# A hybrid decoder layer on one core: index transposes two blocks further behind, two more table blocks ahead, and a reordered last stage

## The chip, the core and the metric

The kernel runs on one core of a Trainium2 chip. The metric is device time in microseconds of one execution, and the median over several executions is compared. In the profile PE is the matmul engine (TensorE) and PEld its weight loads, DVE is VectorE, ACT is ScalarE, POOL is GpSimd, SP is the engine that issues most of the table loads.

## The reference, cut to what matters

The layer is an attention and recurrence mixer followed by PEER, a retrieval of single-neuron experts: each of 256 tokens picks, for each of 8 heads, 16 of 16,384 experts, and mixes their rows. The change touches only PEER and the final RMSNorm.

```python
q = (xt @ w_q).reshape(n, PEER_HEADS, 2, PEER_QDIM // 2)
s = jnp.einsum('nhpd,phkd->nhpk', q, sub_keys)
s1, i1 = lax.top_k(s[:, :, 0], K)          # K = 16 of 128 keys, twice
s2, i2 = lax.top_k(s[:, :, 1], K)
comb = s1[..., :, None] + s2[..., None, :]
cand = i1[..., :, None] * PEER_NKEYS + i2[..., None, :]
top_s, pos = lax.top_k(comb, K)
experts = jnp.take_along_axis(cand, pos, axis=-1)
gate = jax.nn.softmax(top_s, axis=-1)
a = jax.nn.gelu(jnp.einsum('nd,nhkd->nhk', xc, u_tab[ec]))
y = jnp.einsum('nhk,nhkd->nd', gc * a, v_tab[ec])
x = x + gt_f * y
out = x * rsqrt(mean(x * x) + EPS) * g_final
```

## The kernel before, in words

**Dense tokens and sparse tokens.** For the first 160 tokens (`DT`) the kernel computes all experts. The u table (128 blocks of 512 KB, each 128x1024 floats) is multiplied block by block with the layer input, which gives `pu`; a GELU goes into the large tile `W`; `W` is multiplied by a matrix of gates; then the v table (128 more blocks) is multiplied by `W` into `Y`. For the last 96 tokens, in two groups of 64 and 32 (`SPARSE`), expert rows are gathered: 96 gathers of 128 rows (512 KB each) from the u table, then 96 from the v table, issued on POOL into four buffers (`gat`), three ahead. DVE reduces each gathered u tile to one number per row (L1116), and adds each gathered v tile, scaled, into `hrow` (L1125 and L1127), one `hrow` for each group.

**The two loops.** The u loop and the v loop each run over k = 0 to 127. In each step PE does 8 matmuls of 128x160 with one table block. Table loads are issued by `table_ahead()`, one in a step, mostly on SP and about one in five on ACT; ten buffers (tags `raw` and `hl`) go round, and some early blocks have tiles of their own (`GB`, `tab2`, `tab3`).

**Work beside the u loop.** A chain of generators (`work`) holds the DVE work of choosing experts: `topk(1)`, `gates(1)`, `topk(0)`, `gates(0)`, `g_phase`. In each step `spend(work, more)` takes pieces from it until the costs that the pieces yield have used up an allowance of 2.5, less 1.27 for each gather step of that loop step; an overdraft or a remainder carries over. Gather steps come at 0.75 for each u step (`RATE`) and at one for each v step. This order in the program is the order in each engine's queue; an engine takes its instructions in order.

`gates(tt)` normalises the gates on DVE (its last operation is L1048), and then has PE transpose the two index tiles and the gate tile of 128 tokens (`pidx`, L1057 to L1059). `g_phase` builds one-hot matrices from the transposed indices on DVE and ACT (`od`, `oe`, `oa`, `ob`), multiplies them on PE (`pG`), and multiplies the result into `W` (L1167).

**The last stage.** After the v loop `fold` matmuls add the two groups' `hrow` into `Y`. For each of 8 tiles j: fold (PE), gate and residual `x2` (DVE, L1356), square (ACT, L1358), two transposes to rows (PE, L1347), and column sums of squares through matmuls with a column of ones (PE, `psq`). Then come the inverse root (L185 to L192), the scaling, and four stores.

Of the kernel before, what the change touches and what calls it, by code (L numbers as in the profile page):

```python
# [11 lines left out]
F32 = mybir.dt.float32  # L12
# [5 lines left out]
OP = mybir.AluOpType  # L18
AX = mybir.AxisListType

P = 128
# [58 lines left out]
def hybrid_block(ctx: ExitStack, tc: tile.TileContext, A):  # L80
# [47 lines left out]
    def ps(name):  # L128
        return psum.tile([P, 512], F32, name=name, tag="s", bufs=2)
# [618 lines left out]
    def table_ahead():  # L748

        n = len(held)  # L750
        if n >= len(tabs):
            return
        i = turn[n]
        if 6 <= i < 10:

            if i % 2 == 0:
                extra[0] = base.tile([P, 2, WMAX], F32, name="tab2", tag="H", bufs=2)
            r = extra[0][:, i % 2]
        elif 18 <= i < 22:

            r = extra[1].tile([P, WMAX], F32, name="tab3", tag=("oa", "ob")[i % 2], bufs=2)
        else:
            tag = "raw" if (n - (4 if n < 14 else 22)) % 10 in (0, 1, 2, 6) else "hl"
            r = stream.tile([P, WMAX], F32, name="tab", tag=tag, bufs=4 if tag == "raw" else HL)
        (nc.scalar if i >= 32 and i % 5 == 1 else nc.sync).dma_start(r, tabs[i])
        held[i] = r
# [275 lines left out]
    def gates(tt):  # L1042
        s = slice(tt * P, (tt + 1) * P)
        sel, g, gs = mine[tt][7].rearrange("p (a n) -> p a n", a=2), mine[tt][8].rearrange("p (h k) -> p h k", h=8), mine[tt][9]
        nc.vector.tensor_reduce(gs, g, axis=AX.X, op=OP.add)
        nc.vector.reciprocal(gs, gs)
        nc.vector.tensor_scalar(gs, gs, GS, None, op0=OP.mult)
        nc.vector.tensor_tensor(g, g, gs[:, :, None].to_broadcast([P, 8, 16]), op=OP.mult)  # L1048
        yield 0.6
        if tt == NT - 1:  # L1050
            for i, w in enumerate(SPARSE):
                nc.vector.tensor_copy(own[i][:, 1],
                                      g.rearrange("p h k -> p (h k)").rearrange("p (j g) -> p g j", g=P // w))
            spread(1, 0, 1)
        yield 1.4
        pt = ps("pidx").rearrange("p (a t) -> p a t", a=4)
        nc.tensor.transpose(pt[:, 0], sel[:, 0], ident)  # L1057
        nc.tensor.transpose(pt[:, 1], sel[:, 1], ident)
        nc.tensor.transpose(pt[:, 2], g.rearrange("p h k -> p (h k)"), ident)  # L1059
        yield 0.0  # L1060
        nc.scalar.activation(n1T[:, s], pt[:, 0], AF.Copy, scale=-1.0)
        nc.scalar.copy(i2T[:, s], pt[:, 1])
        nc.scalar.copy(gth[:, s], pt[:, 2])
        yield 1.4
        nc.vector.tensor_tensor(gtl[:, s], pt[:, 2], gth[:, s], op=OP.subtract)
        yield 0.3
# [191 lines left out]
    for k in range(P):  # L1258
# [3 lines left out]
        for dt in range(ND):  # L1262
            mm(o[:, k % 2], r[:, dt * P:(dt + 1) * P], h2[:, dt, :DT], dt == 0, dt == ND - 1)
        if k == 7:
            while len(held) < 22:
                table_ahead()
        if k == 8:
            while len(held) < 24:
                table_ahead()
        if 10 <= k < 18 or k >= 22:  # L1270
            table_ahead()
        if k % 2:
            gelu(k - 1, o)
# [47 lines left out]
    out_sb = tail[:, 3072:5120].rearrange("p (a c) -> p a c", a=NT)  # L1321
    sq = tail[:, 5120:7168].rearrange("p (a t) -> p a t", a=ND)
    st = pe.tile([P, 32], F32, name="st")
    for k in range(P):
        for j in range(ND):
            part(j, k, k == 0 and j % 2 == 0, k == P - 1)
        table_ahead()
        due[0] += 1.0
        while due[0] >= 1:
            due[0] -= 1  # L1330
            advance(rows)
        if k == 40:
            nc.sync.dma_start(gfin, bass.AP(tensor=A["g_final"].tensor, offset=A["g_final"].offset,
                                            ap=[[0, P], [1, D]]))
            preload(AF.Abs_reciprocal_sqrt)
# [10 lines left out]
                R[n, b] = (pa if n == 0 else ps)("pr").rearrange("p (a c) -> p a c", a=4)  # L1346
            nc.tensor.transpose(R[n, b][:, j % 4], x2[:, j, n * P:(n + 1) * P], ident)  # L1347

    def sums_of(i):
        for n in range(NT):  # L1350
            mm(psq[:, n:n + 1], sq[:, order[i], n * P:(n + 1) * P], ones[:, 0:1], i == 0 and n == 0, i == ND - 1)

    for i, j in enumerate(order):
        for g, n in enumerate(SPARSE):
            mm(Y[j // 2][:, j % 2, t_of[g]:t_of[g] + n], hrow[g][:, j * P:(j + 1) * P], fold[g], False, True)
        nc.vector.scalar_tensor_tensor(x2[:, j], Y[j // 2][:, j % 2], mod[:, 5, j:j + 1], xT[:, j], op0=OP.mult,  # L1356
                                       op1=OP.add)
        nc.scalar.activation(sq[:, j], x2[:, j], AF.Square)  # L1358
        if i == 2:
            psq = py("psq")  # L1360
        if i > 0:
            rows_of(i - 1)
        if i == 4:
            sums_of(0)
        if i > 3:
            sums_of(i - 3)
        if i == 5:
            for n in range(NT):
                nc.vector.tensor_tensor(out_sb[:, n, :512], R[n, 0].rearrange("p a c -> p (a c)"), gfin[:, :512],
                                        op=OP.mult)  # L1370
    rows_of(ND - 1)
    for i in (5, 6, 7):
        sums_of(i)
    ms, r, t = (st[:, 2 * i:2 * i + 2] for i in range(3))
    rsqrt_to(r, ms, t, psq[:, 0:NT], 1.0 / D)
    for n in range(NT):
# [86 lines left out]
```

## Time and profile before

| | us |
|---|---|
| median of 3 runs (lowest, highest) | 947.3 (947.17, 953.04) |
| the profiled execution's own time | 949.38 |
| its span, first to last instruction | 947.4 |
| PE busy in it | 916.0 |
| DVE busy in it | 642.6 |

The profiled execution took 1.98 us more than its span, and 2.1 us more than the median. The span falls into the mixer and the query projection (0 to some 324 us), the u loop (324 to 637), the v loop (637 to 919) and the last stage (919 to 947). Times in the rows below count from the span's start.

### The profile page before, as it was taken

To read this page: it belongs to the slowest core of one execution; us is meant where nothing else is said; L and a number is where in the kernel's file an instruction comes from. 1 tells how busy PE (TensorE), PEld (TensorE's weight loads), DVE (VectorE), ACT (ScalarE), POOL (GpSimd) and SP (SyncE) were. 2 spreads that over 40 slices of the span, in tenths; PEclk is the share of its full clock that TensorE was granted. 3 is DMA by queue.
4 is the path that set the end of the run, shared out by engine and by line. 5 is a ranking of instruction groups with operands and counts; after the bars stand their busy time and mean duration, and the time that the engine had idled before them with its cause. 6 is when DMAs were issued, how large, how long until landed. Compare 5 with 4: busy or idle time off the path is not lost.

```text
span 947.4 us, 17397 instructions
## 1 busy us (share of the span) xinstructions
PE 916.0 (97%) x6794; PEld 884.1 (93%) x6794; DVE 642.6 (68%) x1428; ACT 313.6 (33%) x693; POOL 216.9 (23%) x233
## 2 busy tenths in 40 slices
PE   6999999999999999999799999999999999999986
PEld 5899988779998999999799999999999999999986
DVE  7798848866878979888978888454444444444453
ACT  4384338865554522101487765010000000000002
POOL 1000000000001023632432333333333333333330
PEclk8999969999999999999899999999999999999995
DMA  9878445246659879899999999999999999999981
GB/s 351 335 267 257 171 131 181 89 141 239 204 180 381 324 270 355 306 418 418 341 373 347 360 337 369 406 417 419 419 417 419 418 419 419 419 417 419 418 325 44
DMA packets 86193, 306.43 MB, mean 323 GB/s; under 512 B 9984, under 2 KB 10464, under 8 KB 85984
## 3 DMA queue, kind: packets, MB, share of 16 engines
q1 hardware_dynamic: 50256, 176.24, 49.5%
q0 software_dynamic: 29520, 106.02, 28.8%
q10 hardware_dynamic: 6336, 23.07, 6.1%
q8 instruction: 53, 0.87, 0.4%
q14 instruction: 28, 0.23, 0.1%
HBM read 304.14 MB, written 1.05 MB: 322 GB/s over the span
## 4 chain that ended last, share of the span: by engine, by line
PE 44%; DMA 29%; DVE 13%; issue 9%; POOL 3%; ACT 0%; DVEq 0%; POOLq 0%; SPq 0%; ACTq 0%
DMA gat<-in_v_row_dram,pairs 24%; PE pu L118 10%; PE col L118 9%; DMA gat<-in_u_row_dram,pairs 5%; PE row L118 4%; PE pq L118 4%; POOL gat L1090 3%; DVE hrow L1127 3%; DVE gat L1116 3%; PE pout L118 2%; PE pbr L118 2%; PE po L118 2%; PE pS L118 2%; PE pG L118 1%; PE ph L118 1%
## 5 line engine op out<-in xcount | busy, mean ns | idle before, releaser
L118 PE MATMUL Y<-gb,tab 128*128 128x160 f32 x2048 | 280.6, 299 | 1.1 <-DMA tab<-in_v_row_dram 0.9
L118 PEld LDWEIGHTS Y<-gb,tab 128*128 128x128 f32 x2048 | 278.5, 190 | 3.2 <-DMA tab<-in_v_row_dram 2.0
L118 PE MATMUL pu<-h,tab 128*128 128x160 f32 x1984 | 278.3, 301 | 0.0
L118 PEld LDWEIGHTS pu<-h,tab 128*128 128x128 f32 x1984 | 272.7, 191 | 0.0
L1127 DVE SCALAR_TENSOR_TENSOR hrow<-gat,act,hrow 128x1024 f32<-128x1024 f32 x94 | 120.7, 1284 | 140.5 <-DMA gat<-in_v_row_dram,pairs 140.4
L1090 POOL DMA_INDIRECT gat<-in_u_row_dram,pairs x96 | 107.1, 1115 | 183.8 <-DVE gat L1116 132.3
L1116 DVE SCALAR_TENSOR_TENSOR gat<-gat,hrow 128x1024 f32<-128x1024 f32 x96 | 116.3, 1220 | 28.7 <-DMA gat<-in_u_row_dram,pairs 24.0
L1090 POOL DMA_INDIRECT gat<-in_v_row_dram,pairs x96 | 90.8, 946 | 181.6 <-DVE hrow L1127 170.2
L100 DVE TENSOR_TENSOR lo<-raw,hi 128x1024 fp32r<-128x1024 f32 (+2 forms) x67 | 80.5, 1206 | 17.8 <-ACT hi L99 17.8
L99 ACT CAST hi<-raw 128x1024 fp32r<-128x1024 f32 (+2 forms) x67 | 68.8, 1036 | 29.3 <-DMA raw<-in_w_vg_dram 5.5
L1358 ACT ACTIVATE gb<-gb 128x256 f32<-128x256 f32 x8 | 3.3, 416 | 209.9 <-DVE gb L1356 209.9
L908 POOL DMA_DIRECT2D gb<-in_keys_dram x1 | 0.7, 720 | 278.3 <-ACT gb L1213 278.3
L1197 ACT ACTIVATE gb<-pu 128x320 f32<-128x320 f32 (+17 forms) x52 | 20.0, 384 | 99.4 <-PE pu L118 95.1
L166 DVE SCALAR_TENSOR_TENSOR raw<-raw,crow 128x1024 f32<-128x1024 f32 x40 | 48.6, 1220 | 5.9 <-DMA raw<-in_ada_t_dram 5.8
L1148 ACT ACTIVATE od<-iota,n1T 128x128 f16<-128x128 f16 x160 | 49.6, 432 | 5.9 <-PE pu L118 5.9
L118 PE MATMUL col<-hlo,hi 128*128 128x256 f32 x160 | 40.8, 289 | 0.0
L118 PE MATMUL col<-hh,hi 128*128 128x256 f32 x160 | 40.2, 286 | 0.0
L118 PE MATMUL col<-xr,wf 128*128 128x256 f32 x128 | 30.6, 405 | 4.3 <-ACT xr L271 4.3
L118 PEld LDWEIGHTS col<-xr,wf 128*128 128x128 f32 x128 | 26.1, 205 | 8.7 <-ACT xr L271 4.7
L118 PEld LDWEIGHTS col<-hh,hi 128*128 128x128 f32 x160 | 30.1, 188 | 2.5 <-issue 2.4
L118 PE MATMUL pq<-hx,hi 128*128 128x258 f32 x128 | 31.7, 290 | 0.0
L118 PEld LDWEIGHTS col<-hlo,hi 128*128 128x128 f32 x160 | 30.2, 189 | 1.0 <-issue 1.0
(342 smaller groups left out, 1320.5 us busy)
## 6 DMA issues: line engine op xcount, KB each, us to landing
tab<-in_u_dram SPq DMA_DIRECT2D x105, 512.0 KB, 7.3
tab<-in_v_row_dram SPq DMA_DIRECT2D x103, 512.0 KB, 16.5
raw<-in_ada_t_dram SPq DMA_DIRECT2D x40, 512.0 KB, 4.7
tab<-in_v_row_dram ACTq DMA_DIRECT2D x25, 512.0 KB, 7.9
raw<-in_w_col_dram SPq DMA_DIRECT2D x20, 512.0 KB, 4.1
tab<-in_u_dram ACTq DMA_DIRECT2D x19, 512.0 KB, 7.2
raw<-in_w_pq_dram SPq DMA_DIRECT2D x16, 512.0 KB, 5.1
raw<-in_w_row_dram SPq DMA_DIRECT2D x12, 512.0 KB, 4.6
```

The source lines that it names most:

```text
L99: nc.scalar.copy(hi, src)
L100: trail = lambda: nc.vector.tensor_tensor(lo, src, hi.bitcast(F32), op=OP.subtract)
L118: nc.tensor.matmul(out, l, r, start=start, stop=stop, skip_group_check=True)
L166: nc.vector.scalar_tensor_tensor(r, r, 1.0, crow, op0=OP.mult, op1=OP.mult, accum_out=mod[:, k, j:j + 1])
L908: nc.gpsimd.dma_start(keys, A["keys"])
L1090: nc.gpsimd.indirect_dma_start(out=r, out_offset=None, in_=A[table], in_offset=bass.IndirectOffsetOnAxis(ap=pairs[:, 0, j:j + 1].bitcast(U ...
L1116: nc.vector.scalar_tensor_tensor(r, r, 1.0, hrow[group_of[j]], op0=OP.mult, op1=OP.mult, accum_out=act[:, 0, j:j + 1])
L1127: nc.vector.scalar_tensor_tensor(acc, r, act[:, 1, j:j + 1], acc, op0=OP.mult, op1=OP.add)
L1148: nc.scalar.activation(od[:, t // 2, :, t % 2], iota[:, :, 0], AF.Abs, bias=n1T[:, c * TC + t:c * TC + t + 1])
L1197: nc.scalar.activation(W[:, k:k + 2, nd:], o[:, :, nd:], AF.Gelu_apprx_tanh)
L1358: nc.scalar.activation(sq[:, j], x2[:, j], AF.Square)
```

## The change

Four edits are made together.

First, `gates` yields 2.0 twice more before its transposes, for both halves of the tokens, which spends 4.0 of allowance with no work in it. Second, blocks 22 and 23 of the u table get two tiles of their own (`tab4`), so that at steps 7 and 8 the loads run up to block 25 instead of 23; the one-a-step loads then pause from step 18 to 23 instead of 18 to 21. Third, the fold of the first group moves into the last 8 steps of the v loop, one tile j in a step. Fourth, the squares of the 8 tiles are added up on DVE into one tile, and two matmuls with the column of ones at the end take the place of sixteen.

```diff
--- before.py
+++ after.py
@@ -756,11 +756,13 @@
             if i % 2 == 0:
                 extra[0] = base.tile([P, 2, WMAX], F32, name="tab2", tag="H", bufs=2)
             r = extra[0][:, i % 2]
+        elif 22 <= i < 24:
+            r = extra[1].tile([P, WMAX], F32, name="tab4", tag="tab4", bufs=2)
         elif 18 <= i < 22:
 
             r = extra[1].tile([P, WMAX], F32, name="tab3", tag=("oa", "ob")[i % 2], bufs=2)
         else:
-            tag = "raw" if (n - (4 if n < 14 else 22)) % 10 in (0, 1, 2, 6) else "hl"
+            tag = "raw" if (n - (4 if n < 14 else 24)) % 10 in (0, 1, 2, 6) else "hl"
             r = stream.tile([P, WMAX], F32, name="tab", tag=tag, bufs=4 if tag == "raw" else HL)
         (nc.scalar if i >= 32 and i % 5 == 1 else nc.sync).dma_start(r, tabs[i])
         held[i] = r
@@ -1053,6 +1055,8 @@
                                       g.rearrange("p h k -> p (h k)").rearrange("p (j g) -> p g j", g=P // w))
             spread(1, 0, 1)
         yield 1.4
+        yield 2.0
+        yield 2.0
         pt = ps("pidx").rearrange("p (a t) -> p a t", a=4)
         nc.tensor.transpose(pt[:, 0], sel[:, 0], ident)
         nc.tensor.transpose(pt[:, 1], sel[:, 1], ident)
@@ -1262,12 +1266,12 @@
         for dt in range(ND):
             mm(o[:, k % 2], r[:, dt * P:(dt + 1) * P], h2[:, dt, :DT], dt == 0, dt == ND - 1)
         if k == 7:
-            while len(held) < 22:
+            while len(held) < 24:
                 table_ahead()
         if k == 8:
-            while len(held) < 24:
+            while len(held) < 26:
                 table_ahead()
-        if 10 <= k < 18 or k >= 22:
+        if 10 <= k < 18 or k >= 24:
             table_ahead()
         if k % 2:
             gelu(k - 1, o)
@@ -1321,7 +1325,16 @@
     out_sb = tail[:, 3072:5120].rearrange("p (a c) -> p a c", a=NT)
     sq = tail[:, 5120:7168].rearrange("p (a t) -> p a t", a=ND)
     st = pe.tile([P, 32], F32, name="st")
+    def fold_in(g, j, last):
+
+        n = SPARSE[g]
+        mm(Y[j // 2][:, j % 2, t_of[g]:t_of[g] + n], hrow[g][:, j * P:(j + 1) * P], fold[g], False, last)
+
     for k in range(P):
+        if k >= P - 8:
+
+            for g in range(len(SPARSE) - 1):
+                fold_in(g, k - P + 8, True)
         for j in range(ND):
             part(j, k, k == 0 and j % 2 == 0, k == P - 1)
         table_ahead()
@@ -1346,31 +1359,24 @@
                 R[n, b] = (pa if n == 0 else ps)("pr").rearrange("p (a c) -> p a c", a=4)
             nc.tensor.transpose(R[n, b][:, j % 4], x2[:, j, n * P:(n + 1) * P], ident)
 
-    def sums_of(i):
-        for n in range(NT):
-            mm(psq[:, n:n + 1], sq[:, order[i], n * P:(n + 1) * P], ones[:, 0:1], i == 0 and n == 0, i == ND - 1)
-
     for i, j in enumerate(order):
-        for g, n in enumerate(SPARSE):
-            mm(Y[j // 2][:, j % 2, t_of[g]:t_of[g] + n], hrow[g][:, j * P:(j + 1) * P], fold[g], False, True)
+        fold_in(len(SPARSE) - 1, j, True)
         nc.vector.scalar_tensor_tensor(x2[:, j], Y[j // 2][:, j % 2], mod[:, 5, j:j + 1], xT[:, j], op0=OP.mult,
                                        op1=OP.add)
-        nc.scalar.activation(sq[:, j], x2[:, j], AF.Square)
-        if i == 2:
-            psq = py("psq")
+        nc.scalar.activation(sq[:, i], x2[:, j], AF.Square)
         if i > 0:
             rows_of(i - 1)
-        if i == 4:
-            sums_of(0)
-        if i > 3:
-            sums_of(i - 3)
+        if i > 1:
+            nc.vector.tensor_tensor(sq[:, 0], sq[:, 0], sq[:, i - 1], op=OP.add)
         if i == 5:
             for n in range(NT):
                 nc.vector.tensor_tensor(out_sb[:, n, :512], R[n, 0].rearrange("p a c -> p (a c)"), gfin[:, :512],
                                         op=OP.mult)
     rows_of(ND - 1)
-    for i in (5, 6, 7):
-        sums_of(i)
+    nc.vector.tensor_tensor(sq[:, 0], sq[:, 0], sq[:, ND - 1], op=OP.add)
+    psq = py("psq")
+    for n in range(NT):
+        mm(psq[:, n:n + 1], sq[:, 0, n * P:(n + 1) * P], ones[:, 0:1], n == 0, True)
     ms, r, t = (st[:, 2 * i:2 * i + 2] for i in range(3))
     rsqrt_to(r, ms, t, psq[:, 0:NT], 1.0 / D)
     for n in range(NT):
```

On PE at the two places of the index transposes, before (`pu` are matmuls of the u loop, 8 for a step; `pidx` are the transposes):

```order
L118 MATMUL pu<-h_2989,tab 128x160 x40
L1057 MATMUL pidx<-ident,gb 128x128
L1058 MATMUL pidx<-ident,gb 128x128
L1059 MATMUL pidx<-ident,gb 128x128
L118 MATMUL pu<-h_2989,tab 128x160 x248
L1057 MATMUL pidx<-ident,gb 128x128
L1058 MATMUL pidx<-ident,gb 128x128
L1059 MATMUL pidx<-ident,gb 128x128
L118 MATMUL pu<-h_2989,tab 128x160 x32
```

and now:

```order
L118 MATMUL pu<-h_2989,tab 128x160 x48
L1061 MATMUL pidx<-ident,gb 128x128
L1062 MATMUL pidx<-ident,gb 128x128
L1063 MATMUL pidx<-ident,gb 128x128
L118 MATMUL pu<-h_2989,tab 128x160 x264
L1061 MATMUL pidx<-ident,gb 128x128
L1062 MATMUL pidx<-ident,gb 128x128
L1063 MATMUL pidx<-ident,gb 128x128
L118 MATMUL pu<-h_2989,tab 128x160 x32
```

The first transposes stand behind three more steps (24 matmuls: x8 and x8 for blocks 22 and 23, which now have tile names of their own ahead of these rows, and x48 for x40), and the second behind two more again (x264 for x248), so five in all.

On DVE, from the end of the choice of experts for tokens 0 to 127 to the first one-hot matrix, before (`gat,act` is the gather step L1116; `gtl` is the first operation that needs the transposes; `oe` and `ob` make the first one-hot matrices):

```order
L1116 SCALAR_TENSOR_TENSOR gat,act<-gat,hrow_3003 128x1024
L1038 TENSOR_TENSOR gb<-gb 128x128
L1045 TENSOR_REDUCE gb<-gb 128x8
L1046 RECIPROCAL gb<-gb 128x8
L1047 TENSOR_SCALAR gb<-gb 128x8
L1048 TENSOR_TENSOR gb<-gb 128x128
L1116 SCALAR_TENSOR_TENSOR gat,act<-gat,hrow_3003 128x1024 x2
L1065 TENSOR_TENSOR gtl<-pidx,gth 128x128
L1151 TENSOR_TENSOR oe<-iota,i2T 128x1024
L1153 TENSOR_TENSOR ob<-oe,gth 128x1024
L1116 SCALAR_TENSOR_TENSOR gat,act<-gat,hrow_3003 128x1024
L1155 TENSOR_TENSOR ob<-oe,gtl 128x1024
```

and now:

```order
L1040 TENSOR_TENSOR gb<-gb 128x128
L1047 TENSOR_REDUCE gb<-gb 128x8
L1048 RECIPROCAL gb<-gb 128x8
L1049 TENSOR_SCALAR gb<-gb 128x8
L1050 TENSOR_TENSOR gb<-gb 128x128
L1120 SCALAR_TENSOR_TENSOR gat,act<-gat,hrow_3003 128x1024 x4
L1069 TENSOR_TENSOR gtl<-pidx,gth 128x128
L1155 TENSOR_TENSOR oe<-iota,i2T 128x1024
L1157 TENSOR_TENSOR ob<-oe,gth 128x1024
L1120 SCALAR_TENSOR_TENSOR gat,act<-gat,hrow_3003 128x1024
L1159 TENSOR_TENSOR ob<-oe,gtl 128x1024
```

The last operation ahead of the third transpose, 128x128 at L1048 (now L1050), has 34 gather steps ahead of it in the whole queue before and 36 now. Between it and `gtl` stand four gather steps, where there were two.

On PE at the end of the v loop, before (`fold_3004` with `hrow_3002` is the group of 64, `fold_3005` with `hrow_3003` the group of 32, `pr` the transposes to rows):

```order
L118 MATMUL Y_6403<-fold_3004,hrow_3002 128x64
L118 MATMUL Y_6403<-fold_3005,hrow_3003 128x32
L118 MATMUL Y_6404<-fold_3004,hrow_3002 128x64
L118 MATMUL Y_6404<-fold_3005,hrow_3003 128x32
L1347 MATMUL pr<-ident,gb 128x128 x2
L118 MATMUL Y_6403<-fold_3004,hrow_3002 128x64
L118 MATMUL Y_6403<-fold_3005,hrow_3003 128x32
L1347 MATMUL pr<-ident,gb 128x128 x2
L118 MATMUL Y_6404<-fold_3004,hrow_3002 128x64
L118 MATMUL Y_6404<-fold_3005,hrow_3003 128x32
L1347 MATMUL pr<-ident,gb 128x128 x2
L118 MATMUL Y_6405<-fold_3004,hrow_3002 128x64
```

and now:

```order
L118 MATMUL Y_6400<-fold_3004,hrow_3002 128x64
L118 MATMUL Y_6397<-gb,tab 128x160 x2
L118 MATMUL Y_6398<-gb,tab 128x160 x2
L118 MATMUL Y_6399<-gb,tab 128x160 x2
L118 MATMUL Y_6400<-gb,tab 128x160 x2
L118 MATMUL Y_6397<-fold_3005,hrow_3003 128x32
L118 MATMUL Y_6398<-fold_3005,hrow_3003 128x32
L1360 MATMUL pr<-ident,gb 128x128 x2
L118 MATMUL Y_6397<-fold_3005,hrow_3003 128x32
L1360 MATMUL pr<-ident,gb 128x128 x2
L118 MATMUL Y_6398<-fold_3005,hrow_3003 128x32
L1360 MATMUL pr<-ident,gb 128x128 x2
```

Each tile's fold after the loop is one matmul instead of two, and no `psq` matmul stands between the tiles; two come at the very end, where six stood. On DVE an add of two 128x256 tiles stands behind each of tiles 2 to 7's gating, and one more at the end.

## Rows read from the trace of the kernel before

**Rows 1.** Waits of PE, whole span: waiter, line, whom; total us, times, longest.

```profile
PE Y L118 <- DVE hrow L1127: 5.2, 1, 5.2
...
PE pidx L1059 <- DVE gb L1048: 3.1, 2, 2.5
...
PE pidx L1058 <- DVE gb L1026: 2.8, 1, 2.8
```

**Rows 2.** Windows by stage: us, busy us (instructions) of PE to POOL, PE clock, DMA share, GB/s.

```profile
395.00:457.00 62.00, 62.00 (x459) 62.00 (x458) 52.89 (x211) 7.40 (x15) 20.54 (x21) 1.00 1.01 405
457.00:475.00 18.00, 12.75 (x85) 12.26 (x84) 16.09 (x31) 9.61 (x25) 8.26 (x7) 0.81 0.90 319
475.00:600.00 125.00, 125.00 (x1095) 124.28 (x1093) 99.34 (x190) 84.60 (x249) 41.11 (x36) 1.00 0.96 358
600.00:700.00 100.00, 100.00 (x739) 100.00 (x738) 46.24 (x66) 4.22 (x10) 35.74 (x35) 1.00 1.03 419
800.00:900.00 100.00, 98.86 (x713) 96.81 (x712) 45.08 (x36) 0.00 (x0) 32.95 (x36) 1.00 1.03 418
```

**Rows 3.** Timeline at the second index transposes: start, us, engine, line, operation.

```profile
457.54 0.27 PE L1057 MATMUL pidx<-ident,gb 128*128 128x128 f32 x1
...
463.04 0.29 DVE L1048 TENSOR_TENSOR gb<-gb 128x128 f32<-128x128 f32 x1
463.25 1.22 DVE L1116 SCALAR_TENSOR_TENSOR gat<-gat,hrow 128x1024 f32<-128x1024 f32 x1
...
463.66 10.85 PE L118 MATMUL pu<-h,tab 128*128 128x160 f32 x64
...
468.27 0.69 DVE L1155 TENSOR_TENSOR ob<-oe,gtl 128x1024 f16<-128x1024 f16 x1
...
474.35 1.08 PE L118 MATMUL pG<-ob,oa 128*128 128x128 f16 x16
```

**Rows 4.** Windows of 2 us, same columns: after that stall, and in the last stage.

```profile
466.00:468.00 2.00, 2.00 (x10) 2.00 (x10) 1.91 (x3) 0.96 (x4) 1.70 (x2) 0.57 0.55 100
926.00:928.00 2.00, 2.00 (x13) 2.00 (x11) 0.81 (x2) 0.83 (x2) 0.00 (x0) 0.50 0.00 0
```

**Rows 5.** Chain that ended last: start, us, link; a u block, a gather, its last step.

```profile
324.72 2.18 PE pu L118 x16
...
894.69 9.58 DMA gat<-in_v_row_dram,pairs
...
922.98 1.29 DVE hrow L1127
```

**Rows 6.** Waits of DVE, 395 to 457 us.

```profile
DVE gat L1116 <- DMA gat<-in_u_row_dram,pairs: 8.8, 7, 2.2
```

**Rows 7.** Waits of SP's queue, 475 to 600 us.

```profile
SPq L765 <- PE pu L118: 109.9, 39, 4.9
```

**Rows 8.** Timeline of the last stage: start, us, engine, line, operation.

```profile
918.80 0.33 PE L118 MATMUL Y<-fold,hrow 128*128 128x64 f32 x2
...
924.32 1.49 PE L118 MATMUL Y<-fold,hrow 128*128 128x32 f32 x6 [5.18 <-DVE hrow L1127]
924.99 0.48 DVE L1356 SCALAR_TENSOR_TENSOR gb<-Y,mod,xT 128x256 f32<-128x256 f32 x1 [0.73 <-PE Y L118]
925.51 0.42 ACT L1358 ACTIVATE gb<-gb 128x256 f32<-128x256 f32 x1 [201.50 <-DVE gb L1356]
...
932.64 1.28 DVE L1369 TENSOR_TENSOR gb<-pr,gb 128x512 f32<-128x512 f32 x2
...
936.30 0.48 DVE L1356 SCALAR_TENSOR_TENSOR gb<-Y,mod,xT 128x256 f32<-128x256 f32 x1 [1.54 <-PE Y L118]
...
937.71 2.56 PE L118 MATMUL psq<-ones,gb 128*128 128x1 f32 x12
940.30 0.16 DVE L185 TENSOR_SCALAR st<-psq 128x2 f32<-128x2 f32 x1 [3.52 <-PE psq L118]
```

**Rows 9.** Groups by line and form: an add of two 128x256 tiles on DVE.

```profile
L864 DVE TENSOR_TENSOR sqa<-sqa,sq 128x256 f32<-128x256 f32 x6 | 2.5, 418 | 0.0
```


## The prediction

> **What bounds the kernel now.** I read the waits of PE first, since PE is busy in 916.0 of 947.4 us: only what stops it, or stretches its work, can be won. From the u loop on three waits matter [rows 1]: 5.2 us at the first fold that needs the last gathered rows, and 2.8 and 3.1 us at the index transposes. Of the 3.1 us the longest is 2.5, so the first pair of transposes cost 0.6 us and the second pair 5.3.
>
> Next come the windows by stage [rows 2]. From 395 to 457 us PE is full and the transfers run at 405 GB/s. From 457 to 475 us PE does 12.75 us of work in 18, its granted clock falls to a mean of 0.81, and the transfers fall to 319 GB/s. From 475 to 600 us PE is full and the transfers run at 358; from 600 us on at 418 to 419. In the u and v loops PE, not a transfer, sets the time until some 800 us: 739 matmul records in 100 us before, 713 from 800 to 900.
>
> The timeline at the stall [rows 3] and the 2 us windows [rows 4] show its second half. PE reaches the transposes at 457.54 and waits for DVE, whose last operation for them starts at 463.04. The 64 matmuls behind them then take 10.85 us, where a block of 16 takes 2.18 [rows 5], so 64 should take 8.7: 2.15 us are lost to a clock that still stands at 0.57 in the window from 466 to 468 us, after the idle time.
>
> Last, the chain [rows 5]: in the v loop it is a string of gathers (the one at 894.69 took 9.58 us) and DVE steps that ends with the DVE step at 922.98. That step ends at 924.27, which I call T. PE waits for it, and what follows T is the last stage.
>
> **The change part by part.**
>
> *The two added yields.* They remove the waits, as far as PE now arrives later than DVE. At stake are 0.6 + 5.3 + 2.15 = 8.05 us. PE reaches the second transposes 0.6 us earlier and five blocks later: 457.54 - 0.6 + 5 x 2.18 = 467.8. DVE has two more gather steps ahead of its last operation (36 for 34). If DVE is bound by its own work, each costs 1.22 us [rows 3]: ready at 463.33 + 2.4 = 465.8, so no wait. If each waits for its gather, the pace is 100 us for the 35 gathers that POOL issues in the window from 600 us [rows 2], 2.86 us: ready at 469.0, a wait of 1.2. In the 62 us ahead, DVE waited for gathers 8.8 us in all [rows 6], so I stay near the first end: 0.2 us.
>
> The waiting instruction moves on to the next place. The first `pG` comes four blocks behind the transposes on PE, now at 467.8 + 0.7 + 8.7 = 477.2. DVE needed 5.6 us from L1048's end (463.33) to the end of L1155 (468.96) with three gather steps in it, and was 5.4 us ahead of PE. Now there are five: 5.6 + 2 x 1.22 = 8.0, ready at 473.8, 3.4 us ahead. At the gathers' pace it is 5.6 - 3 x 1.22 + 5 x 2.86 = 16.2, ready at 482, 4.8 us late. I take 0.8 us, again near the first end. What is queued behind on DVE is the whole gate phase, for which PE waits in turn, but DVE is busy 99.3 of 125 us there [rows 2] and can catch up. So the yields win 8.05 - 0.2 - 0.8 = 7.0 us, with ends of 8.05 and 8.05 - 1.2 - 4.8 = 2.0.
>
> Does T follow? In the u loop the gather steps stand between the loop's own operations, so they come earlier when PE does. In the gate phase the transfers wait, not PE: SP's queue spends 109.9 us of 125 waiting for matmuls of the u loop to free a buffer [rows 7]. So the 358 GB/s there is what was asked for, and there is room up to the 419 seen later. I count T as 7.0 us earlier.
>
> *The two blocks ahead.* Two transfers of 512 KB come some steps earlier, and the pause in loads grows from 4 steps to 6. From step 24 on each step issues the same load as before, ten blocks ahead; that lead hides the pause. It is worth nothing by itself; without that cover, 1 MB at 419 GB/s is 2.5 us, as a gain (bytes moved before the loops are short of them) or a loss (the first gathers behind them), and I keep both ends.
>
> *The fold in the v loop.* Eight folds of 0.33 us [rows 8] add 2.6 us to PE ahead of T. PE waits 5.2 us there, which hides them; without that wait they would cost 2.6. The first group's rows are complete some 30 gathers ahead of T, so these folds wait for nothing.
>
> *The last stage.* From T to L185 it takes 940.30 - 924.27 = 16.0 us [rows 8]. Its matmuls run at half the clock (0.50) [rows 4]; six passes take 1.49 us, 0.25 each. Sixteen fold passes and 28 of the 32 `psq` passes leave it: each tile now needs two fold passes and two transposes, 1.0 us on PE. DVE has 0.48 for the gating and 0.42 for the add [rows 9], 0.9. Nothing else is late in a tile: the square on ACT takes 0.42. On DVE's account the last gating ends at T + 0.6 + 8 x 0.48 + 5 x 0.42 + 1.28 (the two multiplies) = T + 7.8; then square and add, 0.84, and four passes of `psq` at the rate of 12 in 2.56, 0.85: L185 at T + 9.5, a gain of 6.5. At worst the tiles keep their present pace (936.30 - 924.99 = 11.3 us for seven), and only the end shrinks, from 3.5 us to 0.42 + 0.42 + 0.85 + 0.2 = 1.9: a gain of 1.6. PE's and DVE's accounts are both near 8 us and hand over to each other at each tile, so I take 5.2, nearer to the first.
>
> *Sum.* 7.0 + 0 + 0 + 5.2 = 12.2 us. Against the profiled execution's own 949.38 us (1.98 of it outside the span) this is 937.2. That execution stands 2.1 us above the median of the three runs, and the same 12.2 us off 947.3 gives **935.1**.
>
> **The rivals.**
>
> *A: the transfers give part of it back.* If the gate phase cannot move more than its 358 GB/s, the time won by PE is not won by the gathers. From 457 to 600 us the kernel moves 18 x 319 + 125 x 358 = 50.5 MB. With 7.0 us less, 11 us at 405 and 125 at 358 move 49.2 MB; the 1.3 MB left over cost 3.1 us at 419, all of it ahead of T. The time is then 935.1 + 3.1 = 938.2. Against it speaks SP's queue [rows 7]; for it, a DMA share of 0.96 at that rate.
> The Trainium skill, page "DMA: Bandwidth & Descriptors", section Specifications, gives about 358 GB/s as the limit of HBM for one core, which would make this rival the forecast. The trace does not agree: it shows 419 GB/s over 100 us [rows 2].
>
> *B: DVE is still late.* DVE runs at the gathers' pace, the first `pG` waits 4.8 us, and the clock falls as it did after the wait for the second transposes, 2.15 us more. The yields then win 8.05 - 1.2 - 4.8 - 2.15, which is nothing, and 5.2 remains: 942.1. For it: DVE was 5 us behind when PE came, and that wait let it catch up. Against it: the 8.8 us of waits in 62.
>
> *C: slower.* The stall let the table loads catch up. Without it PE meets a v block that has not landed again and again, and each wait long enough for the clock to fall costs like the one at 457.54: 5.3 + 2.15 = 7.45 us. The 12.2 us are gone after 1.6 such waits; three make 935.1 + 3 x 7.45 = 957.4. It needs single waits in the v loop like the 2.8 and 2.5 us there. From 800 us on PE already runs a little short (713 records for 739), but its idle time is 1.1 us of 100 [rows 2].
>
> *D: the last stage gains only its end*, 1.6 for 5.2: 938.7.
>
> **How the numbers follow.** The forecast gets 0.64, A 0.13, B 0.11, D 0.08, C 0.04. The range reaches from 932.0 (most of the 8.05, the last stage at its 6.5) to 942.0 (B); the 2.5 us of the two blocks lie inside it on either side of 935.1. One per cent is 9.5 us, about what a measurement of this kernel can tell from no change. The forecast lies beyond it with 2.7 us to spare and could lose a little of its 0.64 to the middle; A and D lie at 9.1 and 8.6, just inside, and could fall on either side. Faster by over 1%: 0.68; within 1%: 0.28; slower: 0.04.
>
> **What would show it.** The waits of PE should have no entry for the transposes over 1 us, and the granted clock should stay at 1.00 through the u loop. The transfers should run above 400 GB/s where they now drop to 319. A wait of PE at `pG` for `ob` would be B. The last gather step should end near 917 (A: near 920). From there to L185 it should be some 11 us; if it is over 14, D. A wait of PE in front of a table block of over 1 us in the v loop would be C, and would make the prediction wrong, as would a wait at the folds in the last eight steps.

## The result, and the profile after

| | before | after |
|---|---|---|
| median, us (lowest, highest; runs) | 949.61 (947.17, 953.04; 4) | 937.73 (936.92, 941.02; 4) |
| ratio, 95% interval | | 0.9891 [0.9855, 0.9927] |
| profiled execution's own time, us | 949.38 | 941.02 |
| its span, us | 947.4 | 939.1 |

The changed kernel is 1.1% faster; the interval reaches 0.9927, so whether the gain is over one per cent is not settled. The forecast was 935.1 us, within 932.0 to 942.0, and the measured 937.73 lies inside. Of the 2.6 us between the two, 2.3 come from the starting point: the forecast was taken off 947.3 us, the median of three runs of before, and with a fourth run it is 949.61. The profiled execution of after is the slowest of its four. Its u loop began at 327.3 us, 2.75 us later than in the profile of before, though no instruction ahead of that point was changed; where the u loop of the other three began is not on record. So I compare the stages from a mark inside the span: u0, the start of the first u block.

The waits of PE in the profile of after, the biggest ones from the u loop on (waiter, line, whom; total us, times, longest):

```profile
PE Y L118 <- DVE hrow L1131: 2.6, 1, 2.6
PE pu L118 <- ACT gb L1201: 2.4, 1, 2.4
...
PE pr L1360 <- DVE gb L1364: 1.5, 3, 0.9
PE Y L118 <- DMA tab<-in_v_row_dram: 0.9, 4, 0.4
```

Against [rows 1], both entries for the index transposes (`pidx`) are gone, and none for `pG` has come. In their place stands one that no part of the prediction named: 2.4 us for a GELU on ACT (L1201). The wait for the last gathered rows went from 5.2 to 2.6 us.

The windows by stage of after, with the columns of [rows 2]:

```profile
457.00:475.00 18.00, 15.61 (x104) 15.37 (x103) 15.80 (x30) 4.08 (x6) 9.38 (x8) 0.91 1.02 411
475.00:600.00 125.00, 125.00 (x1100) 124.24 (x1099) 104.84 (x197) 91.21 (x268) 42.54 (x38) 1.00 0.97 362
600.00:700.00 100.00, 100.00 (x738) 100.00 (x737) 46.34 (x66) 4.22 (x10) 36.09 (x36) 1.00 1.02 414
800.00:900.00 100.00, 98.94 (x713) 96.83 (x713) 44.43 (x35) 0.00 (x0) 33.40 (x36) 1.00 1.03 418
```

From 457 to 475 us the transfers now run at 411 GB/s for 319, and PE works 15.6 us of 18 for 12.75. The stall has shrunk but is not gone: 2.4 us are idle, and the clock's mean is 0.91.

The timeline of after shows where (start, us, engine, line, operation, and in brackets the idle time before it and who ended it):

```profile
460.12 1.28 ACT L1041 ACT_TABLE_LOAD   x1
...
468.28 0.29 DVE L1040 TENSOR_TENSOR gb<-gb 128x128 f32<-128x128 f32 x1
468.60 0.31 ACT L1041 ACTIVATE gb<-gb 128x128 f32<-128x128 f32 x1 [7.20 <-DVE gb L1040]
...
468.93 1.28 ACT L1201 ACT_TABLE_LOAD   x1
...
470.22 0.77 ACT L1201 ACTIVATE gb<-pu 128x320 f32<-128x320 f32 x2
...
470.71 4.11 PE L118 MATMUL pu<-h,tab 128*128 128x160 f32 x16 [2.39 <-ACT gb L1201]
...
474.66 0.27 PE L1061 MATMUL pidx<-ident,gb 128*128 128x128 f32 x1
...
477.27 0.28 DVE L1069 TENSOR_TENSOR gtl<-pidx,gth 128x128 f16<-128x128 f32 x1
...
483.69 1.08 PE L118 MATMUL pG<-ob,oa 128*128 128x128 f16 x16
```

It is to be read upwards from PE's row at 470.71. PE's next u block needs a `pu` tile in PSUM, the memory that PE writes its results to. There are two such tiles, each for two blocks, and a tile is free when the GELU has read it. The GELU stands on ACT behind the exponential of the gates for tokens 0 to 127 (L1041). ACT takes its instructions in order, has loaded its table at 460.12, and then sits for 7.20 us until DVE has written the exponential's input (468.28 + 0.29 = 468.57). After the exponential it loads the GELU's table, 1.28 us, and only then frees the tile. The transposes (474.66; they stand five blocks further back, not two as the title has it) and the first `pG` (483.69), the two places that the prediction had thought of, have no wait in brackets.

Windows of 2 us of after, same columns, show what the stop left behind:

```profile
468.00:470.00 2.00, 0.32 (x3) 0.07 (x1) 1.52 (x7) 1.38 (x2) 0.00 (x0) 1.00 1.03 422
470.00:472.00 2.00, 1.29 (x5) 1.29 (x6) 2.00 (x3) 0.97 (x3) 0.59 (x1) 0.73 1.03 422
472.00:474.00 2.00, 2.00 (x9) 2.00 (x9) 1.52 (x4) 0.00 (x0) 1.70 (x2) 0.50 1.02 404
```

PE stands still mostly from 468 to 470 us; behind that the granted clock falls to 0.50, its lower level of 1.2 GHz, and 16 matmuls take 4.11 us. In a second execution of the same kernel (e7 below) PE stopped at the same place for 1.25 us, and the clock stayed at 1.00 (a timeline row, then windows of 2 us):

```profile
465.48 2.44 PE L118 MATMUL pu<-h,tab 128*128 128x160 f32 x16 [1.25 <-ACT gb L1201]
```

```profile
464.00:466.00 2.00, 0.75 (x6) 0.52 (x5) 1.90 (x6) 1.74 (x3) 0.00 (x0) 1.00 1.03 420
466.00:468.00 2.00, 2.00 (x18) 2.00 (x17) 1.57 (x3) 0.00 (x0) 1.68 (x1) 1.00 1.03 420
```

The same 16 matmuls took 2.44 us there. So the stop in after cost 2.39 + 1.67 = 4.1 us, and behind the shorter one no slow clock was added.

The end of the v loop and the last stage in the timeline of after:

```profile
905.68 0.33 PE L118 MATMUL Y<-fold,hrow 128*128 128x64 f32 x2
...
905.85 2.39 PE L118 MATMUL Y<-gb,tab 128*128 128x160 f32 x16
...
921.46 1.29 DVE L1131 SCALAR_TENSOR_TENSOR hrow<-gat,act,hrow 128x1024 f32<-128x1024 f32 x1 [0.26 <-DMA gat<-in_v_row_dram,pairs]
...
922.80 0.63 PE L118 MATMUL Y<-fold,hrow 128*128 128x32 f32 x4 [2.58 <-DVE hrow L1131]
...
930.37 0.43 DVE L1376 TENSOR_TENSOR gb<-gb 128x256 f32<-128x256 f32 x1
...
930.94 0.98 PE L118 MATMUL psq<-ones,gb 128*128 128x1 f32 x4 [0.31 <-DVE gb L1376]
931.96 0.16 DVE L185 TENSOR_SCALAR st<-psq 128x2 f32<-128x2 f32 x1 [1.17 <-PE psq L118]
```

The folds of the first group stand between the v blocks, one every 2.4 us. T is now 921.46 + 1.29 = 922.75, and L185 starts 9.2 us behind it, for 16.0 in [rows 8].

Put together, from u0: T came 4.3 us earlier (599.7 to 595.4 us) and the last stage is 6.8 us shorter, 11.1 in all. The span shows 8.3 of it, because u0 itself lay 2.75 us later.

### The profile page after: what moved, and what is told of

It reads as the page before. It is cut to its first block, busy times and chain, and to the rows that moved or that the text cites. A ratio compares the mean times of both kernels' runs of the same rounds, so it can differ in the third digit from the quotient of the medians.

```text
span 939.1 us, 17343 instructions
## 1 busy us (share of the span) xinstructions
PE 911.6 (97%) x6766; PEld 877.2 (93%) x6766; DVE 644.2 (69%) x1432; ACT 313.2 (33%) x693; POOL 219.0 (23%) x233
## 4 chain that ended last, share of the span: by engine, by line
PE 40%; DMA 31%; DVE 16%; issue 8%; POOL 3%; ACT 1%; DVEq 0%; POOLq 0%; ACTq 0%; SPq 0%
DMA gat<-in_v_row_dram,pairs 24%; PE pu L118 11%; PE col L118 8%; DMA gat<-in_u_row_dram,pairs 4%; DVE gat L1120 3%; DVE hrow L1131 3%; PE row L118 3%; POOL gat L1094 3%; PE pout L118 2%; PE pbr L118 2%; PE pq L118 2%; PE po L118 2%; PE pS L118 2%; PE pG L118 1%; PE ph L118 1%
## 5 line engine op out<-in xcount | busy, mean ns | idle before, releaser
L1094 POOL DMA_INDIRECT gat<-in_u_row_dram,pairs x96 | 110.1, 1147 | 178.8 <-DVE gat L1120 124.9
L1201 ACT ACTIVATE gb<-pu 128x320 f32<-128x320 f32 (+18 forms) x55 | 21.0, 385 | 103.8 <-PE pu L118 103.8
```

Source lines behind the costliest of these rows:

```text
L1094: nc.gpsimd.indirect_dma_start(out=r, out_offset=None, in_=A[table], in_offset=bass.IndirectOffsetOnAxis(ap=pairs[:, 0, j:j + 1].bitcast(U ...
L1201: nc.scalar.activation(W[:, k:k + 2, nd:], o[:, :, nd:], AF.Gelu_apprx_tanh)
```

## The experiments

All rows of this table come from one profiled execution of each kernel, read in the same way: u0, then T from u0, PE's wait for that GELU, T to L185, and u0 to L185, which leaves out what the start of the u loop adds. The ratios are to before on the same chip. One execution is a small sample: e1, e5 and e6 have the u loop of before unchanged, and yet their T − u0 lies 0.7 to 1.9 us below that of before.

| kernel | u0 | T − u0 | wait for GELU | T to L185 | u0 to L185 | ratio, 95% interval |
|---|---|---|---|---|---|---|
| before | 324.6 | 599.7 | none | 16.0 | 615.7 | |
| after | 327.3 | 595.4 | 2.4 | 9.2 | 604.7 | 0.9891 [0.9855, 0.9927] |
| e1_last_stage | 325.6 | 599.0 | none | 9.2 | 608.2 | 0.9922 [0.9895, 0.9949] |
| e2_yields_blocks | 327.6 | 591.3 | 0.4 | 14.9 | 606.2 | 0.9959 [0.9936, 0.9981] |
| e3_yields_only | 323.5 | 593.3 | 1.8 | 16.0 | 609.3 | 0.9951 [0.9927, 0.9975] |
| e4_exp_later | 324.4 | 591.2 | none | 9.6 | 600.8 | 0.9898 [0.9871, 0.9925] |
| e5_squares_only | 330.1 | 597.9 | none | 11.5 | 609.4 | 0.9971 [0.9953, 0.9988] |
| e6_fold_only | 326.3 | 597.8 | none | 13.3 | 611.1 | 0.9984 [0.9962, 1.0006] |
| e7_after_again | 323.2 | 593.0 | 1.2 | 9.8 | 602.8 | 0.9908 [0.9869, 0.9946] |
| e8_exp_later_rate | 325.7 | 587.2 | none | 16.9 | 604.1 | 0.9920 [0.9894, 0.9945] |
| e9_rate775_yields2 | 321.1 | 592.3 | none | 9.9 | 602.2 | 0.9943 [0.9907, 0.9978] |
| e10_rate80_yields3 | 325.9 | 592.2 | none | 14.2 | 606.3 | 0.9975 [0.9944, 1.0005] |
| e11_exp_later_again | 327.9 | 590.9 | none | 9.6 | 600.5 | 0.9894 [0.9849, 0.9939] |

My theory from the profile of after (W) is that the yields won less than forecast because PE now stops behind ACT's exponential, and that T follows PE's time in the u loop. Its rivals are that the transfers or the gathers hold T back (A of the prediction, and, for the later runs, that the pace at which the program asks for gathers does: G), and that the last stage's two edits, or the two added blocks, give or take something else than forecast.

**The last stage alone**, before with the third and fourth edit:

```diff
+        if k >= P - 8:
+            for g in range(len(SPARSE) - 1):
+                fold_in(g, k - P + 8, True)
...
+        if i > 1:
+            nc.vector.tensor_tensor(sq[:, 0], sq[:, 0], sq[:, i - 1], op=OP.add)
```

> The kernel before with the two edits of the last stage alone (first fold in the v loop, squares added on DVE). In the profile of the changed kernel the stretch from the last gather step to the sum's first use took 9.2 us for 16.0. If that edit is worth what this stretch shows and nothing else moves, this run is 6.8 us faster than before (0.7 per cent); by the prediction's term it is 5.2. If the folds in the v loop delay the last gather, it is less than 4. PE's wait for the transposes should still be 5.3 to 6 us.

T to L185 took 9.2 us and the time fell by 0.78%, 7.4 us of 948.8. T from u0 stayed (599.0 for 599.7), so the folds in the loop cost nothing on the way to T; PE's wait for the last rows shrank instead, to 2.3 us. The waits at the transposes came to 5.1 us, a little under what I expected. The interval (4.8 to 10.0 us) does not tell 6.8 from 5.2.

**The yields with the two blocks**, before with the first and second edit:

```diff
+        elif 22 <= i < 24:
+            r = extra[1].tile([P, WMAX], F32, name="tab4", tag="tab4", bufs=2)
...
         yield 1.4
+        yield 2.0
+        yield 2.0
```

> The kernel before with the yields and the two more blocks, the last stage as before. Theory W (a new wait): the exponential on ACT stands ahead of the GELU that frees the matmuls' PSUM bank, and waits for DVE; PE stops 2.4 us there and then runs 16 matmuls at 4.1 us for 2.2; 3.7 us faster than before. Rival R (transfers hold the last gather): PE gains 3 to 4 us in the u loop, but the last gather step moves by 1.5 us or less. The prediction's term was 7.0.

T came 8.4 us earlier, against R, with a wait for the GELU of only 0.4 us. The time fell by 0.41%, 3.9 us (1.8 to 6.1 by the interval). That is near W's 3.7, but the profiled execution does not bear out W's sum: its wait was short, and its 9.5 us from u0 to L185 are more than the times allow, so it or the profiled execution of before is not a typical one.

The last stage is that of before, yet it took 14.9 us for 16.0. The granted clock goes with that. In before PE had waited 5.2 us for the last rows, and the clock was 0.50 from T on, as it was in e3 (a wait of 4.6 us, and again 16.0). Here PE had waited 2.5 us, and the clock fell some 2 us behind T, which is 918.89. Windows of before and then of e2:

```profile
924.00:926.00 2.00, 1.68 (x8) 1.69 (x9) 0.90 (x3) 0.42 (x1) 0.00 (x0) 0.50 0.00 0
```

```profile
919.00:921.00 2.00, 1.78 (x16) 1.70 (x17) 1.09 (x3) 0.83 (x2) 0.00 (x0) 1.00 0.00 0
921.00:923.00 2.00, 2.00 (x13) 2.00 (x12) 0.99 (x3) 0.83 (x2) 0.00 (x0) 0.52 0.00 0
```

**The yields alone**, without the blocks:

```diff
         yield 1.4
+        yield 2.0
+        yield 2.0
```

> The yields alone, without the two more blocks. If the blocks are worth nothing, as predicted, the time is that of the run with yields and blocks within 1 us. If the later transposes need the blocks to keep PE fed, PE shows waits for table blocks between 380 and 480 us and the run is 2 to 4 us slower than that one.

The time fell by 0.49%, and the interval covers that of the kernel with the blocks: the two blocks are worth nothing that these runs can see, and PE has no wait for a table block between 380 and 480 us. The new wait is there without the blocks too, so it comes from the yields. In the waits of PE of this kernel:

```profile
PE Y L118 <- DVE hrow L1129: 4.6, 1, 4.6
PE pu L118 <- ACT gb L1199: 1.8, 1, 1.8
```

**The squares alone** (both folds stay at the end) and **the fold alone** (the sums through `psq` stay):

```diff
-        if i == 4:
-            sums_of(0)
-        if i > 3:
-            sums_of(i - 3)
+        if i > 1:
+            nc.vector.tensor_tensor(sq[:, 0], sq[:, 0], sq[:, i - 1], op=OP.add)
```

> The kernel before with the squares added on DVE alone; both folds stay in the last stage. If the column sums on PE set the last stage's pace, the stretch from the last gather step to the sum's first use falls from 16.0 to some 11 us (four fold passes and two transposes for each tile, 1.2 us each, then 0.8 for the sums). If the folds set it, it stays above 13.

```diff
+        if k >= P - 8:
+            for g in range(len(SPARSE) - 1):
+                fold_in(g, k - P + 8, True)
```

> The kernel before with the first fold in the v loop alone; the column sums stay on PE. The last eight blocks of the v loop take 0.2 to 0.3 us more each, hidden as long as PE still waits for the last gather step. If the folds set the last stage's pace, its stretch falls from 16.0 to some 12 us; if the column sums do, it stays above 13.5.

From T to L185 they took 11.5 and 13.3 us: 4.6 and 2.7 us less than before, 7.3 in sum, where both together gave 6.8. The fold alone lies between the 12 and the 13.5 us that I had set for the two readings; the squares gave more, so the column sums on PE held the last stage back more than the folds did. In the fold's kernel the `psq` matmuls stay between the tiles, and twelve records of them are left at the end, as in [rows 8]:

```profile
934.72 2.56 PE L118 MATMUL psq<-ones,gb 128*128 128x1 f32 x12
937.31 0.16 DVE L185 TENSOR_SCALAR st<-psq 128x2 f32<-128x2 f32 x1 [3.52 <-PE psq L118]
```

By time the squares gained 0.29%; the fold's interval reaches 1, so a gain of the fold alone is not shown by time.

**After once more**, unchanged, to see what of it repeats:

> The changed kernel once more, unaltered, beside the next three on one chip. If the parts add up, 7.4 us (last stage alone) and 4.0 us (yields and blocks alone) give 11.4 us off the kernel before. Its profile tells how far PE's wait of 2.4 us behind the exponential differs between executions: in the run of the yields with the blocks it was 0.4 us, in that of the yields alone 1.8.

In this execution PE waited 1.2 us for the GELU and T came 593.0 us after u0, so the size of the new wait differs between executions of one kernel. The u loop began 4.1 us earlier than in the first one. The ratio agrees. By time it is 8.7 us off before, and the 11.4 of the parts lies inside the interval (5.1 to 12.4).

**The exponential behind two more yields**, in the half that stalls, on top of after. In the program order GELUs now stand ahead of it on ACT; what stands behind it in `gates` moves back with it:

```diff
+        if tt == 0:
+            yield 2.0
+            yield 2.0
         nc.scalar.activation(g, g, AF.Exp)
```

> The changed kernel, with the exponential of the gates of tokens 0 to 127 put two yields (some three blocks) further back in the program; what it computes is unchanged. Theory W: ACT's wait of 7.2 us for DVE at the exponential shrinks to under 3, PE's wait of 2.4 us for the GELU and the half clock behind it go, and the run is 4.3 us faster than the changed kernel. Rival R: PE's wait goes, but the last gather step and the time stay within 1.5 us. A third reading, that DVE is late as such, has the wait come back at the transposes or at the first product with the one-hot matrices.

> The exponential later alone, once more, as the measure for the two runs beside it. If its gain over the changed kernel is real, no wait of PE for the GELU shows again, and the last gather step stands 591 to 592 us behind the first u block, as it did (changed kernel: 595.4 and 593.0 in two executions).

In both runs the wait is gone, and T comes 591.2 and 590.9 us after u0, 4.2 and 4.6 us earlier than in the first execution of after and 1.8 and 2.1 earlier than in the second. The timeline of the first shows a GELU ahead of the exponential, which now has no wait in brackets; what ACT waits for is PE:

```profile
465.44 0.28 DVE L1040 TENSOR_TENSOR gb<-gb 128x128 f32<-128x128 f32 x1
...
465.82 0.44 ACT L1204 ACTIVATE gb<-pu 128x320 f32<-128x320 f32 x1 [4.29 <-PE pu L118]
466.27 1.28 ACT L1044 ACT_TABLE_LOAD   x1
...
467.56 0.31 ACT L1044 ACTIVATE gb<-gb 128x128 f32<-128x128 f32 x1
...
474.26 8.86 PE L118 MATMUL pu<-h,tab 128*128 128x160 f32 x64
```

That is W's mechanism for the wait, shown by taking its cause away. It did not come back at the transposes, and at a `pG` only with 0.2 and 0.6 us. By time W's 4.3 us did not show, and it is not established that this beats after: 0.9898 and 0.9894 against 0.9891 and 0.9908, with intervals that cover each other. Between the second execution of after and these two the row sums differ by some 2 us, a fifth of a per cent, and the start of the u loop alone varies more than that.

**More gathers for each u step**, on top of e4, since PE still waited 3.8 us for the last rows there:

```diff
-RATE = 0.75
+RATE = 0.8
```

> The changed kernel with the exponential two yields later, and with 0.8 gather steps in each u step instead of 0.75. Theory G: the last gather step sets the end, and the gate phase has transfers to spare (362 of 419 GB/s), so gathers moved there bring the last step forward; five more gathers are done when the v loop begins, PE's wait at the last fold (3.8 us with the exponential later) falls under 1 us, and the time is 2 to 4 us below that of the run with the exponential later. Rival R: the bytes ahead of the end are the same and the transfers are full from 600 us on, so less than 1 us is won.

G was half right. T came 587.2 us after u0, some 8 us before the v loop ended, so that the v loop is the last and not the gathers; the 16.9 us in the table count the 8 us that T lay ahead. But DVE has more gather steps ahead of the gates, and is late again at the transposes (waits of PE):

```profile
PE pidx L1066 <- DVE gb L1053: 4.9, 1, 4.9
```

The time is 0.9920, no better than after.

**A rate between, or the higher rate, with more yields ahead of the transposes**:

```diff
-RATE = 0.75
+RATE = 0.775
...
         yield 2.0
         yield 2.0
+        if tt == 0:
+            yield 2.0
+            yield 2.0
         pt = ps("pidx").rearrange("p (a t) -> p a t", a=4)
```

> The exponential later, 0.775 gather steps in a u step, and two more yields before the second transposes. With 0.8 steps the gathers ended 8 us ahead of PE, and PE waited 4.9 us at the transposes again. If gathers and PE are to end together, this is the place between: PE's wait at the transposes under 1 us, its wait for the last gather step under 2, last gather step 588 to 590 us behind the first block of the u loop (591.2 with the exponential later alone), 2 us faster than that run. If the transfers alone set it, no change.

> The exponential later, 0.8 gather steps, three more yields before the second transposes. If the wait of 4.9 us at the transposes (and the half clock behind it) was all that was wrong with 0.8, PE ends some 588 us behind the first u block instead of 595, and the time is 3 to 4 us below that of the exponential later alone. If DVE cannot do the added gather steps beside the choice of experts, the wait moves on to the products with the one-hot matrices.

(The second has the rate 0.8 and three such yields.) Both moved the wait on to the next place, the first `pG`, which is where rival B had put it, and so both missed what I expected of them: T came 592.3 us after u0 in the first, for 588 to 590, and in the second PE ended the v loop 597.6 us after u0, for 588. (T lay 5.4 us ahead of that end, which is in its 14.2 us in the table.) In the waits of PE, first of the one and then of the other:

```profile
PE pG L118 <- DVE ob L1165: 3.6, 1, 3.6
```

```profile
PE pG L118 <- DVE ob L1164: 6.6, 1, 6.6
```

The second has another wait of 1.5 us at a `pG`. They came to 0.9943 and 0.9975, for after's 0.9891 and, on the same chip, e11's 0.9894: no gain from either. The profiled execution of the first was the fastest of its twelve (932.3 us for a median of 942.1), so its row in the table shows where it waits but does not explain its median.

## Why the prediction was right, and where its terms were off

**The two yields: the mechanism was right, the size off.** The term was 7.0 us, with ends of 2.0 and 8.05. (The lower end joins two readings: at the gathers' pace DVE is ready for the transposes at 469.0 and not at 465.8, so the first `pG` would wait some 7 us and not 4.8, and the end would be near nothing.) T from u0 moved by 4.3 us in the profile of after and by 6.7 in the second execution. The prediction subtracted 0.2 us for a wait left at the transposes and 0.8 for the first `pG`; both measured nothing. What it left out is the wait behind ACT's exponential, 2.4 us and 1.67 of low clock in the one execution, 1.2 in the other. The step that failed is the sentence on the next place to which the wait moves: I followed DVE to its next customer on PE and did not ask what else stands in a queue behind the late DVE. In the kernel before ACT already waited for the same operation, as its timeline shows:

```profile
461.93 0.31 ACT L1039 ACTIVATE gb<-gb 128x128 f32<-128x128 f32 x1 [6.81 <-DVE gb L1038]
```

But there PE was itself held at the transposes, and its next u block started at 463.66 [rows 3], so ACT's wait cost nothing.

The 8.05 us at stake were read from one execution, and other executions of the same u loop had less to lose. In e1, e5 and e6 PE waited 5.1, 3.4 and 4.2 us at the transposes, for 5.9 in before. Their v loops began 312.5, 309.7 and 310.6 us after u0, for 312.6, and that start came at 304.3 to 304.8 in the three with hardly a wait left (e2, e4, e11). So some 5 to 8 us were there to be won. The 2.15 in the 8.05 is a little high as well: 64 matmuls at the full clock take 8.86 us in the same view (e4 at 474.26), which leaves 1.99 of the 10.85.

The rows agree with the account, as far as one execution of each can. In e4 and e11, where the wait is gone, T − u0 is 8.5 and 8.8 us shorter than in before, and 6.6 to 8.1 shorter than in e1, e5 and e6. In after it is 4.2 us longer than in e4, where 2.39 + 1.67 = 4.1 were lost. With a wait of 0.4 us (e2) it is 0.1 longer than in e4, with 1.2 (e7) 1.8, with 1.8 (e3) 2.1. The times do not show all of it: from u0 to L185 e4 and e11 lie 15 us below before, and their ratios give 9.7 and 10.0 us, at most 12.2 and 14.3. Why that is so stays open.

**Does T follow PE?** Yes, and this felled rival A. The v loop began 4.28 us earlier after u0 in after and T came 4.26 us earlier; in e4 it was 8.3 and 8.5. In e5 and e6, with nothing changed in the u loop, the v loop began 3.0 and 2.0 us earlier than in before, and T came 1.8 and 1.9 earlier. The transfers between 457 and 475 us rose to 411 GB/s. In the gate phase SP's queue still waits for PE, as in [rows 7]; from the waits of SP's queue of after, 475 to 600 us:

```profile
SPq L767 <- PE pu L118: 108.1, 39, 4.9
```

The place of T itself would have misled: the prediction named 917 us if it was right and 920 for A, and taken at before's u0 it came at 924.27 − 4.26 = 920.0. It was there for another reason, which only the start of the v loop and the waits tell apart. Another of its signs failed in this execution for the same reason: the clock did not stay at 1.00 through the u loop.

Nor was 358 GB/s a limit of the gate phase: without the stop, e4 moved more in the same window.

```profile
475.00:600.00 125.00, 124.83 (x1097) 123.96 (x1096) 106.39 (x200) 89.67 (x266) 45.79 (x39) 1.00 0.99 375
```

That agrees with the Trainium skill, page "DMA: Bandwidth & Descriptors", section Bandwidth, which gives 425 GB/s for a large transfer into SBUF by a core whose neighbour on the same memory is idle; the trace of after shows 418 from 800 to 900 us.

**The two blocks**: nothing forecast, nothing seen, within the 2.5 us on either side.

**The fold in the v loop**: hidden, as forecast. The last eight blocks take 2.40 us each for 2.18, some 1.8 us in all, and PE's wait for the last rows paid for it.

**The last stage: the size off, to the good side.** The term was 5.2 us, between 1.6 and 6.5; it measured 6.8 in after and e1 and 6.2 to 6.4 in e7, e4 and e11. Part of the 6.8 goes with the clock, as in e2. Against kernels with the same clock it is 6.2 where the clock is 0.50 from T on (e7 and before), and 5.6 where it stays at 1.00 for some 2 us behind T (after and e2). DVE's account alone (L185 at T + 9.5) was the right one: it came at T + 9.2 to 9.8. I had taken less because PE's and DVE's accounts hand over at each tile; but PE has a tile's fold done while DVE still works at the one before: in after DVE's waits for a fold come to 0.8 us in all. Rival D fell.

**The sum**: 12.2 us forecast. From u0 to L185 it measured 11.1 in the first execution of after and 12.9 in the second, and the ratios give 10.4 us (0.0109 of 949.6) and 8.7 (0.0092 of 948.2), with some 3.5 us on either side. A yield term that was too large and a last stage that was too small nearly cancelled, and that was luck.

**The other rivals.** B did not happen in after, but its place is real: it decides as soon as DVE has more gather steps ahead of the gates (e9, e10). C did not happen: the longest wait of PE for a table block in the v loop is 0.4 us. What stays open is how large the new wait is in the mean of many executions; two profiles of after show 1.2 and 2.4 us, and those of e2 and e3, with the same u loop but for the two blocks, 0.4 and 1.8.

## What to carry to other kernels

When a consumer of a late producer is moved back, look in every in-order queue for other instructions that wait for the same producer, and for what is queued behind those: here an eviction of PSUM stood on ACT behind an exponential that DVE fed. A stop of PE can cost more than its length: behind the one of 2.4 us the clock fell to 0.50 and the cost was 4.1 us, while behind those of 1.2 (e7) and 1.8 us (e3) it stayed at 1.00. Where the start of a stage varies between executions by more than the change is worth, read the stages from a common mark inside the span and only then compare the ends. And profile the unchanged kernel more than once: here the same u loop took up to 3 us more or less.

## What was not expected of the hardware

The start of the u loop varied from 321.1 to 330.1 us over the profiled executions, with no change ahead of it. Of the 5.9 us between the spans of the two executions of after it is 4.1, and of the 3.2 between e4 and e11 all. It goes in the main with the granted clock in the mixer, whose mean from 100 to 150 us lies between 0.73 (e11) and 0.90 (e9). The windows of after and then of e9:

```profile
100.00:150.00 50.00, 50.00 (x305) 41.41 (x303) 31.32 (x76) 20.57 (x40) 0.00 (x0) 0.76 0.40 132
```

```profile
100.00:150.00 50.00, 50.00 (x355) 42.92 (x355) 35.74 (x85) 26.60 (x57) 0.00 (x0) 0.90 0.51 166
```

PE counts as busy for all 50 us in both, and yet it was granted 0.76 of its clock in the one and 0.90 in the other, and 305 and 355 matmuls are on record; u0 was 327.3 and 321.1 us. The two do not go together exactly: e5 had 0.76 too, and its u0 was 330.1. The Trainium skill, page "TensorE: Matmul & The Clock Gate", Part 1, says that how many matmuls run slow differs between runs of one kernel. The traces agree with that, by the two clocks above. How much of the 9 us the clock accounts for, and what decides it in this stage, no run here was made to show.
